# A decoder on one core: where the operands of the matrix products lie in SBUF, by pads between pools and wider rows

## The chip, the core and the metric

The kernel runs on one core of a Trainium2 chip. The metric is the time of one execution on the device in microseconds (us); of several executions the median is taken, and less is better. The core has five engines that the text names: TensorE (PE, with its weight loads as PEld), VectorE (DVE), ScalarE (ACT), GpSimd (POOL) and the DMA queue of SyncE (SP). SBUF is the on-chip memory of 128 partitions; a tile occupies the same byte addresses in each of its partitions, and "address" below means the byte address within a partition.

## The reference, cut to what matters

A sequence of 256 tokens of width 1024 goes through four decoder layers (differential attention, latent attention, dilated attention, differential attention, each followed by a gated feed-forward), a norm, and then two layers of a second kind, each a mix of pooling, convolution and sparse attention followed by a feed-forward with a short convolution. Nearly all of the arithmetic is products of activations with weight matrices in float32:

```
for i in range(DEPTH):
    h = rms_norm(x, attn_norm[i])
    mix = attention(h, ...)                       # one of three kinds
    x = x + mix
    x = x + swiglu(rms_norm(x, ffn_norm[i]), f_w_gu[i], f_w_out[i])
...
for l in range(DEPTH_2):
    mix = token_mix(h, ...)
    h = layer_norm(DEEPNORM_ALPHA * h + mix, ln1_g[l], ln1_b[l])
    ffn = conv_ffn(h, w_up[l], ffn_dw_w[l], ffn_dw_b[l], w_down[l])
    h = layer_norm(DEEPNORM_ALPHA * h + ffn, ln2_g[l], ln2_b[l])
```

The second kind's pooling divides windowed sums over 2, 4, 8 and 16 tokens by the number of tokens in the window, which is below the window's width only for the first 15 tokens.

## The kernel before

**Products.** Activations lie transposed, 128 channels by 256 tokens, in eight chunks. Each float32 operand is split into a high and a low part of the type float32r, and a product is three matmuls (`mm3`, L287): high by high, high weights by low activations, low weights by high activations. A matmul holds one operand of 128x128 in the array (the weights in the sense of the PE, loaded by an LDWEIGHTS of its own before each matmul) and streams the other, the moving operand, through it. In most products (`smode`, `smode2`) the model's weights are the held operand and 256 columns of activations move. In `mmode` it is the other way round: 128 tokens of activations are held, and 288 to 512 columns of weights move.

**Operands.** Weights come by `weights` (L295): a DMA of SP brings a piece of up to 128x1024 into `raw`, ACT rounds it into `whi`, DVE subtracts into `wlo` (L308); five buffers of `raw` and six each of `whi` and `wlo` of 4096 bytes rotate. The moving activations are of three kinds. The input of a layer's first products is split into `xh` and `xl` (L382 and L383), each a tile of eight rows of 258 columns, so that row k begins 1032*k bytes into the tile; 256 columns hold x, two more hold a gain and a bias for the early products of `normed` (258 columns wide). Results between products (attention outputs, the hidden rows of the feed-forwards) lie in slots of the pool `big` (tile `s4`, in the trace `s`), four rows of 256 columns each. The pooled and the convolved rows of `token_mix` (`pp` and `cc`, L1555 and L1637) lie in the pool `wk` under the tag `pl`, two rows of 256 columns in a tile.

**Where they lie.** The pools lie one behind the other in the order in which `Program.__init__` opens them (const, w, big, wk, and then the pools of some layers), the tiles of a pool one behind the other, each rounded up to 32 bytes. In the compiled program, taken modulo 512: `xh` begins at 160, so row k at 160+8k; `xl` at 224, so row k at 224+8k; all buffers of `raw`, `whi` and `wlo` at 192; all slots of `big` at 192; the pool `wk` at 192; its tag `pl` at 384. Slices of the weights are whole multiples of 512 bytes into their tile, but for the two weights 288 and 328 columns wide. The distance of a moving operand behind the held one is therefore -32+8k for `xh`, 32+8k for `xl`, 0 for the slots, and 192 for `pp` and `cc`.

**Order.** The instructions of the woven stretches (attention, token mixing) keep an order that a small planner in the program writes out with assumed durations (`US`, L29); addresses don't enter it. Feed-forwards and output projections run as they are written: PE through one block of weights after the other.

**Small things that the change touches.** `pk1` (L405) holds constants, among them `cnt` (2x256 columns), the reciprocal window counts that POOL multiplies in at L1532. `acc` (L1121) sums the moments of the norms, `ang` and `angn` (L1335 and L1338) are the rope's angles in the pool `wk`; the pool `mix` (`self.own`, L1326) is opened for the second kind of layers.

Of the kernel before, what the change touches and what calls it, by code (L numbers as in the profile page):

```python
# [10 lines left out]
F32 = mybir.dt.float32  # L11
R = mybir.dt.float32r
# [7 lines left out]
S = 256  # L20
# [8 lines left out]
US = {256: 0.12, 288: 0.132, 328: 0.155, 384: 0.175, 512: 0.235}  # L29
POOLED = (5, 7)  # L30
NH = 18
WARM = 10
NORM, POOL = (7, 8, 9), 8
FILL = -3.0e38
# [39 lines left out]
class Pack:  # L74
    def __init__(self):
        self.at, self.parts, self.n = {}, [], 0
# [25 lines left out]
def prepare(i):  # L102
    f = lambda a: np.asarray(a)
# [45 lines left out]
    p = Pack()  # L149
# [28 lines left out]
    nat = np.arange(S)  # L178
# [2 lines left out]
    p.add("ropeC", rope_tab(500000.0, 16, sigma()))  # L181
    inv = (10000.0 ** (-np.arange(32, dtype=np.float64) / 32)).astype(np.float32)
    p.add("inv", np.tile(inv[None], (128, 1)))
    cnt = np.zeros((128, 2, S), np.float32)
    for g, win_ in enumerate((2, 4, 8, 16)):
        cnt[(g % 2) * 64:(g % 2) * 64 + 64, g // 2] = np.float32(1) / np.minimum(nat + 1, win_).astype(np.float32)
    p.add("cnt", cnt.reshape(128, 2 * S))
    a["pack"] = np.concatenate(p.parts, axis=1)

    sg = sigma()  # L190
    q, k = sg[:, None], sg[None, :]
# [4 lines left out]
    for t in range(2):  # L196
        h = slice(t * 128, t * 128 + 128)
# [14 lines left out]
class Program:  # L212
    def __init__(self, tc, ins, out, at):
        self.tc, self.nc, self.ins, self.out, self.at = tc, tc.nc, ins, out, at
        self.ready = []
        self.woven, self.now, self.queue, self.inside, self.serial = False, 0.0, [], False, 0
        with ExitStack() as ctx:
            pool = lambda n, b, **k: ctx.enter_context(tc.tile_pool(name=n, bufs=b, **k))
            self.const = pool("const", 1)
            self.wp = pool("w", 3)  # L220
            self.big = pool("big", 12)
            self.wk = pool("wk", 2)
            self.ps = pool("ps", 2, space=bass.MemoryType.PSUM)
            self.pool = pool
            self.main()
# [140 lines left out]
    def setup(self):  # L366
        nc, c = self.nc, self.const
        i = self.ins
        self.x = []
        self.pk0 = c.tile([128, PK0], F32, name="pk0")  # L370
        nc.scalar.dma_start(self.pk0, i["pack"][:, :PK0])
        self.x4 = []
        for h in range(2):
            x = c.tile([128, 4, 256], F32, name=f"x{h}")
            nc.sync.dma_start(x, i["xT"][h])
            if h == 0:
                self.ready.append(self.weights(i["w_aqk"][0, 0, 0], 512))
            self.x4.append(x)
            self.x += [x[:, k, :] for k in range(4)]
            self.x2 = getattr(self, "x2", []) + [x[:, k:k + 2, :] for k in (0, 2)]  # L380
        self.ident = self.col("ident", 0, 128)
        self.xh = c.tile([128, 8, 258], R, name="xh")  # L382
        self.xl = c.tile([128, 8, 258], R, name="xl")  # L383
        self.identr = c.tile([128, 128], R, name="identr")
        nc.vector.tensor_copy(self.identr, self.ident)
        self.ones = c.tile([128, 1], F32, name="ones")
        nc.vector.memset(self.ones, 1.0)
        self.onesd = c.tile([128, 1], F32, name="onesd")
        nc.vector.memset(self.onesd, 1.0 / D)
        self.onesq = c.tile([128, 128], F32, name="onesq")  # L390
        nc.vector.memset(self.onesq, 1.0 / 512)

        self.woven = True
        ps = self.tp_bank()[:, :128]
        for _ in range(WARM):
            self.matmul(ps, self.onesq, self.onesq, start=True, stop=True)
        self.woven = False
        warm = c.tile([128, 1], F32, name="warm")
        self.act(warm, self.ones)
        self.nhalf = c.tile([128, 8], F32, name="nhalf")  # L400
        nc.vector.memset(self.nhalf, -0.5)
# [716 lines left out]
    def moments(self, k, chunk, accs, eng):  # L1118

        if k == 0:  # L1120
            accs.append(self.wk.tile([128, 256], F32, name="acc", tag="acc", bufs=3))  # L1121
            eng.tensor_copy(accs[0], chunk)
        elif k < 7:
            eng.tensor_add(accs[0], accs[0], chunk)  # L1124
        else:
            accs.append(chunk)
# [92 lines left out]
    def early(self, st):  # L1219

        h, l = self.xh, self.xl
        st["z"] = [(h[:, k, :], l[:, k, :]) for k in range(8)]
        for n, name in ((256, st["g"]), (257, st["b"])):
            v = self.col(name, 0, 8)
            self.act(h[:, :, n], v)
            self.nc.vector.tensor_sub(l[:, :, n], v, h[:, :, n].bitcast(F32))
# [95 lines left out]
    def angles(self):  # L1324
        nc = self.nc
        c = self.own = self.pool("mix", 1)  # L1326
        self.causal = c.tile([128, 384], F32, name="causal")
        nc.scalar.dma_start(self.causal, self.ins["causal"])
        pi = c.tile([128, 2], I32, name="posi")
        nc.scalar.dma_start(pi, self.ins["pos"])  # L1330
        pf = c.tile([128, 2], F32, name="posf")
        nc.vector.tensor_copy(pf, pi)
        inv = self.col("inv", 0, 32)
        wk = self.wk
        ang = wk.tile([128, 2, 32], F32, name="ang", bufs=1)  # L1335
        for t in range(2):
            nc.vector.tensor_scalar(ang[:, t, :], inv, pf[:, t:t + 1], None, op0=OP.mult)
        n = wk.tile([128, 2, 32], F32, name="angn", bufs=1)  # L1338
        magic = 12582912.0
        nc.vector.tensor_scalar(n, ang, float(1.0 / (2 * math.pi)), magic, op0=OP.mult, op1=OP.add)  # L1340
        nc.vector.tensor_scalar(n, n, -magic, None, op0=OP.add)
        c1 = 6.28125
        c2 = float(np.float32(2 * math.pi - c1)) 
        c2 = float(np.float32(np.frombuffer(np.uint32(np.frombuffer(np.float32(c2).tobytes(), np.uint32)[0] & 0xFFFFF000).tobytes(), np.float32)[0]))
        c3 = float(np.float32(2 * math.pi - c1 - c2))
        flat = lambda a: a.rearrange("p a b -> p (a b)")
        for cc in (c1, c2, c3):
            self.stt(flat(ang), flat(n), -cc, flat(ang), OP.mult, OP.add)
        lim = 3.1415925
        nc.vector.tensor_scalar(ang, ang, lim, -lim, op0=OP.min, op1=OP.max)  # L1350

        self.rt = c.tile([128, 2, 128], F32, name="rt")
        self.act(self.rt[:, :, 96:128], ang, AF.Sin)
        nc.vector.tensor_scalar(self.rt[:, :, 64:96], self.rt[:, :, 96:128], -1.0, None, op0=OP.mult)
        self.act(n, ang, AF.Abs)
        nc.vector.tensor_scalar(n, n, -1.0, float(math.pi / 2), op0=OP.mult, op1=OP.add)
        self.act(self.rt[:, :, 0:32], n, AF.Sin)
        nc.vector.tensor_copy(self.rt[:, :, 32:64], self.rt[:, :, 0:32])
        self.onesc = c.tile([128, 128], F32, name="onesc")
        nc.vector.memset(self.onesc, 1.0 / 256)  # L1360
        self.pw = c.tile([128, 2, 2, 64], F32, name="pw")
        nc.scalar.dma_start(self.pw, self.ins["pool_w"])
        self.bd = c.tile([128, 2, 128], F32, name="bd")
        nc.vector.memset(self.bd, 0.0)
        self.cvp = c.tile([128, 2, 286], F32, name="cvp")
        nc.vector.memset(self.cvp, 0.0)
        self.zk = [c.tile([128, 2, 256], F32, name=f"zk{n}") for n in range(2)]
        for t in self.zk:
            nc.gpsimd.memset(t, 0.0)
        self.hb = c.tile([128, 2, 26], F32, name="hb")  # L1370
        for l in range(2):
            nc.vector.tensor_scalar(self.hb[:, l, 0:2], self.col(f"bc{l}", 2, 2), 0.5, None, op0=OP.mult)
            nc.vector.tensor_scalar(self.hb[:, l, 2:26], self.col(f"bg{l}", 0, 24), 0.5, None, op0=OP.mult)

    def token_mix(self, l, st):
        nc, wk, i = self.nc, self.wk, self.ins
# [138 lines left out]
        s1 = wk.tile([128, 2, 256], F32, name="pl1", tag="pl", bufs=4)  # L1515
        gp = nc.gpsimd
# [11 lines left out]
        shifted(s0, s1, al, 1, 4)  # L1528
        gp.tensor_copy(s1[lo_, 1, :], s0[lo_, 1, :])
        shifted(s1, s0, hi_, 1, 8)  # L1530
        cnt = self.col("cnt", 0, 512).rearrange("p (f n) -> p f n", f=2)
        gp.tensor_mul(s1, s1, cnt)  # L1532
        gp.tensor_sub(s1, s1, u)
        cvp = self.cvp
        for f in range(2):
# [109 lines left out]
        for f in range(8):  # L1645
# [3 lines left out]
            for s in range(2):  # L1649
                g = gate(3 * f + s)  # L1650
# [3 lines left out]
        for hf in range(2):  # L1654
            w = self.weights(i["w_ato"][l, hf], 512)
            for ff in range(4):
                f = hf * 4 + ff
                ps = self.mm_bank()[:, :256]
                self.smode(ps, w, 0, 4, ff * 128, os_, True, True)
                g = gate(3 * f + 2)  # L1660
# [4 lines left out]
        chunk, st = self.deepnorm(f"ln1_g{l}", f"ln1_b{l}", True)  # L1665
# [3 lines left out]
    def conv_ffn(self, l, st, more):  # L1669
# [9 lines left out]
        for j in range(FC):  # L1679
# [15 lines left out]
            nc.vector.tensor_mul(h, s, u[:, 1, :])  # L1695
            self.split(hs[j][0], hs[j][1], h, 1.0, nc.gpsimd if j < NH else None)
        chunk, st = self.deepnorm(f"ln2_g{l}", f"ln2_b{l}", more)
# [34 lines left out]
```

## Time and profile before

| what | value |
|---|---|
| median of 3 runs | 2299.73 us (2299.43 to 2301.78) |
| profiled execution, its own time | 2302.48 us |
| its span in the trace | 2300.7 us |
| mean granted TensorE clock | 0.985 of 2.4 GHz |
| PE busy | 2226.4 us (97%) |
| DVE busy | 1625.7 us (71%) |
| ACT busy | 1325.1 us (58%) |
| POOL busy | 148.2 us (6%) |
| moved by DMA | 365.93 MB, mean 159 GB/s |

The end of a matmul in the trace is modelled and neighbours overlap, so neither a matmul's duration nor PE's busy share tells how fast the products follow each other. That is read from the starts: the time from the first start to the last, divided by the number of matmuls between, is called the pitch below.

### The profile page before, as it was taken

What the parts mean: (1) busy time and instruction counts of PE and PEld (TensorE: products, weight loads), DVE (VectorE), ACT (ScalarE), POOL (GpSimd) and SP (SyncE); (2) the same over time, 40 slices, a digit from 0 to 9 for tenths busy, and PEclk for the clock granted to TensorE, in tenths of its full rate; (3) what the DMA queues carried; (4) which work ended last, traced back from release to release, by engine and by line L of the source; (5) the groups of instructions that cost most, each with busy time, mean ns of one, the idle gap of its engine ahead of it and who ended that gap; (6) DMA issues with size and microseconds to landing.
All of it is one profiled execution on the core that took longest, in us unless ns stands there. A gap on an engine that the chain in (4) does not pass through costs nothing.

```text
span 2300.7 us, 42530 instructions
## 1 busy us (share of the span) xinstructions
PE 2226.4 (97%) x16676; PEld 2100.6 (91%) x16676; DVE 1625.7 (71%) x2940; ACT 1325.1 (58%) x2378; POOL 148.2 (6%) x167
## 2 busy tenths in 40 slices
PE   9999998999999999999999999989989998998998
PEld 7899997999977778999978999889989998998998
DVE  7776666766556656766677766796888689778875
ACT  7764457544556655644587545645566564656653
POOL 0000000100000000000000001010012011001211
PEclk9999999999999999999999999999999999998999
DMA  6345563355554343455633655534445544443643
GB/s 243 124 155 185 155 184 118 124 189 157 184 193 138 110 138 129 147 184 160 208 125 111 211 169 175 174 136 140 169 139 198 157 153 156 169 161 123 212 155 103
DMA packets 111801, 365.93 MB, mean 159 GB/s; under 512 B 12528, under 2 KB 14704, under 8 KB 111600
## 3 DMA queue, kind: packets, MB, share of 16 engines
q1 hardware_dynamic: 109728, 360.17, 47.6%
q10 hardware_dynamic: 1728, 2.78, 0.4%
q8 instruction: 131, 2.15, 0.4%
q14 instruction: 70, 0.57, 0.1%
q0 software_dynamic: 144, 0.26, 0.1%
HBM read 362.38 MB, written 1.05 MB: 158 GB/s over the span
## 4 chain that ended last, share of the span: by engine, by line
PE 72%; DVE 6%; ACT 4%; issue 1%; DMA 0%; POOL 0%; ACTq 0%; DVEq 0%; POOLq 0%
PE mm L265 62%; PE sc L265 6%; PE tp L319 2%; DVE wlo L308 1%; ACT whi L236 1%; PE tp L265 1%; ACT xh L236 1%; ACT s L236 1%; ACT x L236 1%; DVE score L1481 0%; PE tp L1135 0%; PE tp L728 0%; DVE mx L1480 0%; DVE gut L239 0%; DVE acc L1124 0%
## 5 line engine op out<-in xcount | busy, mean ns | idle before, releaser
L308 DVE TENSOR_TENSOR wlo<-raw,whi 128x1024 fp32r<-128x1024 f32 (+3 forms) x752 | 844.7, 1127 | 355.8 <-ACT whi L236 352.7
L236 ACT ACTIVATE whi<-raw 128x1024 fp32r<-128x1024 f32 (+3 forms) x752 | 731.8, 978 | 589.0 <-PE mm L265 368.5
L265 PE MATMUL mm<-xh,wlo 128*128 128x256 f32 x2496 | 706.5, 283 | 16.5 <-DVE wlo L308 16.5
L265 PE MATMUL mm<-xh,whi 128*128 128x256 f32 x2496 | 713.1, 286 | 0.3 <-ACT whi L236 0.3
L265 PE MATMUL mm<-xl,whi 128*128 128x256 f32 x2496 | 705.5, 283 | 0.4 <-DVE xl L1185 0.3
L265 PE MATMUL mm<-s,whi 128*128 128x256 f32 x2944 | 538.1, 284 | 0.0
L265 PEld LDWEIGHTS mm<-xh,wlo 128*128 128x128 f32 x2496 | 474.6, 190 | 17.4 <-DVE wlo L308 17.4
L265 PEld LDWEIGHTS mm<-xh,whi 128*128 128x128 f32 x2496 | 475.7, 191 | 2.8 <-issue 1.0
L265 PEld LDWEIGHTS mm<-xl,whi 128*128 128x128 f32 x2496 | 475.4, 191 | 1.5 <-DVE xl L1185 0.8
L265 PEld LDWEIGHTS mm<-s,whi 128*128 128x128 f32 x2944 | 460.3, 192 | 2.2 <-issue 1.1
L265 PE MATMUL mm<-s,wlo 128*128 128x256 f32 x1472 | 416.9, 283 | 0.0
L265 PEld LDWEIGHTS mm<-s,wlo 128*128 128x128 f32 x1472 | 282.3, 192 | 0.0
L265 PE MATMUL mm<-whi,xh 128*128 128x512 f32 (+2 forms) x592 | 238.4, 404 | 8.0 <-ACT whi L236 4.5
L265 PE MATMUL mm<-wlo,xh 128*128 128x512 f32 (+2 forms) x592 | 233.9, 395 | 3.5 <-DVE wlo L308 3.5
L265 PE MATMUL mm<-whi,xl 128*128 128x512 f32 (+2 forms) x592 | 232.6, 393 | 0.0
L265 PEld LDWEIGHTS mm<-whi,xh 128*128 128x128 f32 x592 | 113.3, 192 | 30.8 <-ACT whi L236 5.2
L265 PEld LDWEIGHTS mm<-wlo,xh 128*128 128x128 f32 x592 | 113.6, 192 | 24.0 <-DVE wlo L308 4.8
L265 PEld LDWEIGHTS mm<-whi,xl 128*128 128x128 f32 x592 | 113.2, 191 | 22.1
L236 ACT ACTIVATE s<-guh 128x256 fp32r<-128x256 f32 x132 | 54.8, 416 | 100.2 <-DVE guh L552 93.6
L504 POOL TENSOR_TENSOR rstd<-ms,nhalf 128x2 f32<-128x2 f32 x29 | 29.0, 1000 | 1070.0 <-DVE ms L502 1061.5
L548 DVE TENSOR_TENSOR gut<-mm,rbc 128x512 f32<-128x512 f32 x88 | 60.4, 691 | 40.9 <-PE mm L265 40.9
L239 DVE SCALAR_TENSOR_TENSOR gut<-mm,pk,gut 128x255 f32<-128x255 f32 (+1 forms) x160 | 76.1, 477 | 6.1 <-ACT gut L236 3.8
(326 smaller groups left out, 2502.1 us busy)
## 6 DMA issues: line engine op xcount, KB each, us to landing
raw<-w_gu SPq DMA_DIRECT2D x176, 512.0 KB, 3.8
raw<-w_up SPq DMA_DIRECT2D x88, 512.0 KB, 4.0
raw<-w_zs SPq DMA_DIRECT2D x60, 512.0 KB, 4.7
raw<-w_out SPq DMA_DIRECT2D x64, 384.0 KB, 3.2
raw<-w_cqk SPq DMA_DIRECT2D x48, 512.0 KB, 4.3
raw<-w_out SPq DMA_DIRECT2D x64, 320.0 KB, 2.8
raw<-w_aqk SPq DMA_DIRECT2D x32, 512.0 KB, 4.5
raw<-w_cv SPq DMA_DIRECT2D x24, 512.0 KB, 4.0
```

The costliest lines, as they stand in the source:

```text
L236: return self.nc.scalar.activation(out, in_, func, bias=bias, scale=scale, **kw)
L239: return self.nc.vector.scalar_tensor_tensor(out, a, s, b, op0=op0, op1=op1)
L265: i = self.nc.tensor.matmul(*a, **kw)
L308: e.tensor_sub(lo, raw, hi.bitcast(F32))
L319: i = self.nc.tensor.transpose(out, in_, self.ident if ident is None else ident)
L504: self.powered = [self.nc.gpsimd.tensor_tensor(r, ms, self.nhalf[:, :n], op=OP.pow).ins]
L548: nc.vector.tensor_mul(t, ps, rb[:, None, :].to_broadcast([128, 2, 256]))
```

## The change

A tile `padx` of 56 columns (224 bytes) in the pool const ahead of `xh`, and three pools of one unused tile each: 72 columns (288 bytes) ahead of the weights, 48 (192 bytes) ahead of the slots, 80 (320 bytes) ahead of `wk`. The rows of `xh` and `xl` become 384 columns (1536 bytes, three times 512) apart; 258 of them are used as before. `cnt` shrinks to 17 columns per half and POOL's multiplication is made in two parts (16 columns one by one, 240 by the last column broadcast); `acc` moves to the pool `mix`, `ang` and `angn` to the rotating tag `t1`. No product is added, left out or reordered in the program's text.

```diff
+PADS = (56, 72, 48, 80)
...
-    cnt = np.zeros((128, 2, S), np.float32)
+    cnt = np.zeros((128, 2, 17), np.float32)
...
             self.const = pool("const", 1)
+            pad = lambda n, cols: pool(n, 1).tile([128, cols], F32, name=n)
+            pad("padw", PADS[1])
             self.wp = pool("w", 3)
+            pad("padb", PADS[2])
             self.big = pool("big", 12)
+            pad("padk", PADS[3])
             self.wk = pool("wk", 2)
...
-        self.xh = c.tile([128, 8, 258], R, name="xh")
-        self.xl = c.tile([128, 8, 258], R, name="xl")
+        c.tile([128, PADS[0]], F32, name="padx")
+        self.xh = c.tile([128, 8, 384], R, name="xh")
+        self.xl = c.tile([128, 8, 384], R, name="xl")
...
-            accs.append(self.wk.tile([128, 256], F32, name="acc", tag="acc", bufs=3))
+            accs.append(self.own.tile([128, 256], F32, name="acc", tag="acc", bufs=3))
...
-        st["z"] = [(h[:, k, :], l[:, k, :]) for k in range(8)]
+        st["z"] = [(h[:, k, :258], l[:, k, :258]) for k in range(8)]
...
-        ang = wk.tile([128, 2, 32], F32, name="ang", bufs=1)
+        ang = self.t1("ang", (2, 32))
...
-        n = wk.tile([128, 2, 32], F32, name="angn", bufs=1)
+        n = self.t1("angn", (2, 32))
...
-        cnt = self.col("cnt", 0, 512).rearrange("p (f n) -> p f n", f=2)
-        gp.tensor_mul(s1, s1, cnt)
+        cnt = self.col("cnt", 0, 34).rearrange("p (f n) -> p f n", f=2)
+        gp.tensor_mul(s1[:, :, :16], s1[:, :, :16], cnt[:, :, :16])
+        gp.tensor_mul(s1[:, :, 16:], s1[:, :, 16:], cnt[:, :, 16:].to_broadcast([128, 2, 240]))
```

## Rows read from the trace of the kernel before

**Rows 1.** Page, part 1: busy time, share of the span, instructions.
```profile
span 2300.7 us, 42530 instructions
PE 2226.4 (97%) x16676; PEld 2100.6 (91%) x16676; DVE 1625.7 (71%) x2940; ACT 1325.1 (58%) x2378; POOL 148.2 (6%) x167
```

**Rows 2.** Page, part 4: the chain that ended last, by engine.
```profile
PE 72%; DVE 6%; ACT 4%; issue 1%; DMA 0%; POOL 0%; ACTq 0%; DVEq 0%; POOLq 0%
```

**Rows 3.** Pieces of that chain: start us, us, engine, tile, line, instructions.
```profile
437.72 8.94 PE mm L265 x75
...
451.32 169.82 PE mm L265 x1424
...
1271.89 144.74 PE mm L265 x1215
...
2257.04 30.60 PE mm L265 x255
```

**Rows 4.** Stretches: us, engines' busy time (instructions), clock, DMA share, GB/s.
```profile
150.00:300.00 150.00, 150.00 (x1261) 150.00 (x1261) 97.77 (x132) 72.83 (x108) 0.00 (x0) 1.00 0.56 177
1702.00:1840.00 138.00, 137.94 (x1142) 137.79 (x1143) 107.75 (x168) 82.14 (x135) 21.47 (x17) 0.99 0.57 186
```

**Rows 5.** Page, part 5, groups of products: busy us, mean ns, idle before.
```profile
L265 PE MATMUL mm<-xh,wlo 128*128 128x256 f32 x2496 | 706.5, 283 | 16.5 <-DVE wlo L308 16.5
...
L265 PE MATMUL mm<-s,whi 128*128 128x256 f32 x2944 | 538.1, 284 | 0.0
...
L265 PE MATMUL mm<-s,wlo 128*128 128x256 f32 x1472 | 416.9, 283 | 0.0
```

**Rows 6.** Groups by shape, PE, smaller products: busy us, mean ns, idle before.
```profile
L265 PE MATMUL sc<-s,whi 128*128 128x256 f32 x220 | 43.1, 294 | 2.6 <-ACT s L236 1.7 <-DVE s L239 0.5 <-ACT blat L236 0.4
...
L265 PE MATMUL sc<-s,wlo 128*128 128x256 f32 x110 | 31.3, 284 | 0.0
L265 PE MATMUL sc<-xl,whi 128*128 128x258 f32 x96 | 29.9, 311 | 0.0
...
L265 PE MATMUL mm<-pp,whi 128*128 128x256 f32 x64 | 11.7, 276 | 0.0
...
L265 PE MATMUL mm<-pp,wlo 128*128 128x256 f32 x32 | 8.8, 276 | 0.0
```

**Rows 7.** Timeline of PE, second kind's first output stage: `pp` and `cc`.
```profile
1627.84 0.39 PE L265 MATMUL mm<-cc,whi 128*128 128x256 f32 x2
...
1630.10 0.28 PE L265 MATMUL mm<-pp,wlo 128*128 128x256 f32 x1
```

**Rows 8.** Timeline of PE, same stage, some 6 us on: slots.
```profile
1634.10 0.40 PE L265 MATMUL mm<-s,whi 128*128 128x256 f32 x2
...
1636.50 0.28 PE L265 MATMUL mm<-s,wlo 128*128 128x256 f32 x1
```

**Rows 9.** Timeline of PEld in the stretch of rows 7: weight loads.
```profile
1628.07 0.30 PEld L265 LDWEIGHTS mm<-cc,whi 128*128 128x128 f32 x2
1628.29 0.19 PEld L265 LDWEIGHTS mm<-cc,wlo 128*128 128x128 f32 x1
```

**Rows 10.** Groups by shape, PE: products with 512 moving columns of weights.
```profile
L265 PE MATMUL mm<-whi,xh 128*128 128x512 f32 x544 | 222.8, 411 | 8.0 <-ACT whi L236 4.5 <-ACT s L236 2.3 <-ACT qtok L236 1.1
```

**Rows 11.** Waits of PE: for whom, us in total, times, longest.
```profile
PE mm L265 <- DVE wlo L308: 20.0, 6, 6.3
PE tp L1135 <- DVE acc L1124: 5.4, 2, 2.7
```

**Rows 12.** POOL's count multiplication (L1532): duration min/median/max, starts.
```profile
L1532 POOL TENSOR_TENSOR pl<-pl,pk x2: 1214/1215/1216, 1516.7 to 1934.4; 128x512 f32<-128x512 f32 x2
```

**Rows 13.** The tile `angn` on DVE and ACT: first and last use.
```profile
L1340 DVE TENSOR_SCALAR angn<-ang x1: 179/179/179, 1254.1 to 1254.1; 128x64 f32<-128x64 f32 x1
...
L236 ACT ACTIVATE rt<-angn x1: 242/242/242, 1260.9 to 1260.9; 128x64 f32<-128x64 f32 x1
```

More of the change, by code (lines that the diff above doesn't have):

```diff
@@ L183, in prepare @@
     p.add("inv", np.tile(inv[None], (128, 1)))
-    cnt = np.zeros((128, 2, S), np.float32)
+    cnt = np.zeros((128, 2, 17), np.float32)
     for g, win_ in enumerate((2, 4, 8, 16)):
-        cnt[(g % 2) * 64:(g % 2) * 64 + 64, g // 2] = np.float32(1) / np.minimum(nat + 1, win_).astype(np.float32)
-    p.add("cnt", cnt.reshape(128, 2 * S))
+        cnt[(g % 2) * 64:(g % 2) * 64 + 64, g // 2] = np.float32(1) / np.minimum(nat[:17] + 1, win_).astype(np.float32)
+    p.add("cnt", cnt.reshape(128, 34))
     a["pack"] = np.concatenate(p.parts, axis=1)
```

## The prediction

> **What bounds the kernel now.** I read the page's busy times first: PE stands at 97%, DVE at 71%, ACT at 58%, POOL at 6% [rows 1]. Matmul ends are modelled, so 97% alone proves little; the chain of waits settles it: 72% of the span is PE's, 6% DVE's, 4% ACT's [rows 2]. The chain taken in order of time shows where: it runs through PE alone in long pieces, the longest 169.82 us with 1424 matmuls [rows 3]. I counted the pieces of 8.9 us or longer whose matmuls follow each other in under 123 ns: there are 13, with 8299 matmuls, the first and the last in [rows 3]; the chain as shown begins only at 376 us, so the first layer's feed-forward comes from the stretches, 1261 matmuls in 150 us with PE busy throughout and DVE busy 97.77 of 150 us [rows 4]. In these 9560 matmuls nothing but PE's own pace sets the time. What a matmul costs there is the pitch: 144.74 us / 1215 = 119.1 ns where mostly `xh` and `xl` move, 30.60 us / 255 = 120.0 ns where only slots move [rows 3].
>
> **The row that matters.** One stage of the kernel before has both addresses of the change side by side. In the output stage of the first token mixing, `pp` and `cc` lie 192 bytes behind the weights: the starts run from 1627.84 to 1630.10 us, which is 20 matmuls in 2.26 us, 113.0 ns [rows 7]. Six us later slots move at a distance of 0, with the same shape, the same line, the same kind of weight tile: 1634.10 to 1636.50 us, 20 matmuls in 2.40 us, 120.0 ns [rows 8]. Weight loads go on beside the stream in either case (one begins every 0.11 us) [rows 9], so a held operand is read while a moving one is, and the distance between their addresses can matter. I take 113.3 ns for the distance 192 (the printed starts are rounded to 10 ns; the whole run of rows 7 repeats every 0.34 us per three matmuls).
>
> **The change part by part.** First, where things end up. `padx` puts `xh` from 160 to 160+224 = 384 (modulo 512), and with rows of 1536 bytes all eight rows, and those of `xl`, stand at 384. The pool const grows by 224 + 2*4032 bytes and loses 1920 of `cnt`, 6368 in all; with the pad of 288 the weights move by 6656 = 13*512 and stay at 192. The pad of 192 puts the slots at 384, the pad of 320 leaves `wk` at 192 (7168 = 14*512 in all) and `pl` at 384. So every product with 256 moving columns of activations gets the distance 192 that `pp` and `cc` have now; the scores and transposes keep theirs, but for some short ones.
>
> Gain at most. `xh` and `xl` move in 3 * (2496 + 96) = 7776 matmuls [rows 5, 6], at 119.1 - 113.3 = 5.8 ns each: 45.1 us. Slots move in 2944 + 1472 + 220 + 110 = 4746 [rows 5, 6], at 120.0 - 113.3 = 6.7 ns: 31.8 us. Together 76.9 us over 12,522 matmuls.
>
> What of it reaches the end. Of the 9560 matmuls of the stretches in which PE alone sets the time, some 260 are `pp` and `cc` (192 in all, as both have the counts of [rows 6]) and wide ones, so 9300 of 12,522, 74%, give their gain in full: 56.9 us. The other 26% (20.0 us) lie in woven attention and token mixing, where PE waits now and then for DVE and ACT; with PE's 72% of the whole chain I take half, 10.0 us. Does the feed keep up at the new pace? The tightest long stretch is the second kind's feed-forward, with DVE busy 107.75 of 138 us [rows 4]; if PE needs 5.3% less time there, DVE is busy 107.75 of some 131 us, 82%, and the DMA's 186 GB/s become 196 at a share of 0.60 in place of 0.57; I count no loss but keep it as a rival. PE's waits for `wlo` are 20.0 us in six places [rows 11], at the starts of stages; they neither grow nor shrink.
>
> The products of `mmode` change too, and no row shows their new distance: weights at 192 move and activations at 384 are held, which is 512 - 192 = 320. There are 544 with `whi` and `xh`, three times as many in all, 1632 [rows 10]. Nearest are the gains of the narrow products, so I bound each by 6.7 ns either way: 10.9 us, half of it on the path, -5.5 to +5.5 us. I take 0, because nothing in the trace says on which side 320 lies.
>
> The rest is small. POOL's multiplication of 1.215 us [rows 12] becomes two of together the same columns; bounds from nothing to another 1.2 us per layer, on an engine that is idle 94% of the time, and the rows are wanted by PE only with a step queued 34 us later. If that cover were gone, it would be 2.4 us. `acc` keeps its three buffers; PE waits 5.4 us for it in two places [rows 11] and that stays. `ang` and `angn` take two of the six `t1` buffers from 1254 to 1261 us [rows 13]; a later user could wait for them at most those 7 us and has four other buffers first: 0. The smaller `pk1` takes a quarter megabyte off a DMA at the start: 0. No wait is added to any queue.
>
> Sum: 56.9 + 10.0 = 66.9 us, from a profiled span of 2300.7 us to 2233.8 (2235.6 us by that execution's own time of 2302.5). The median of the runs before is 2.8 us under the profiled execution's time, so against the median: 2299.7 - 66.9 = 2232.8, which I give as **2233 us**.
>
> **The rivals.** *No effect.* The pace of `pp` and `cc` comes from something else in their stage, and distance does nothing. For it: they are only 192 products, in two places. Against it: [rows 7, 8] are 6 us apart, on the same engines' work. It gives 2300 us; chance 0.08. The Trainium skill speaks for this rival: "SBUF — State Buffer", section "Who interferes with whom", gives PE two independent read ports, one for the moving operand and one for LDWEIGHTS, and says that PE never waits on anyone. By that rule both pitches would be equal and the sum would be 0; the trace has 113.0 against 120.0 ns [rows 7, 8] and does not agree.
>
> *Slower.* The same premise, and in addition the present drift of 8 bytes from row to row is what makes `xh` (119.1 ns) faster than the slots (120.0 ns) [rows 3]. With all rows at one distance `xh` and `xl` would then go at the slots' pace: 7776 * 0.9 ns = 7.0 us more, 2307 us. It decides from the point at which the distance 192 brings less than 0.9 ns. The chance is 0.06.
>
> *Feed-bound.* DVE's splitting of the weights becomes the bound in the second kind's layers, where it is busiest [rows 4]. Then some 3400 of the 9300 free-running matmuls gain nothing, 20.8 us, and the woven stages' 10.0 us fall away as well: 36.1 us are left, 2264 us. For it stands DVE's 78% in that stretch; against it, that PE doesn't wait for `wlo` inside it [rows 11]. The chance is 0.10.
>
> *More.* All of the 76.9 us arrive, and the wide products gain 5.5 us: 2217 us, chance 0.06.
>
> **How the numbers follow.** The forecast of 2233 us has 0.70, with a range of its own from 2222 to 2247 (woven part all or none, wide products at either bound). The range of 8 in 10 takes in "more" and "feed-bound" and leaves out the 0.14 of no effect and slower, with a little of each tail: 2217 to 2265 us. A measurement of this kernel tells about 0.2% (4.6 us) from no change. Faster: 0.70 + 0.10 + 0.06 = 0.86; within 0.2%: 0.08; slower: 0.06.
>
> **What would show it.** Right: in the timeline after, starts of three `mm` products of `s` lie 0.34 us apart and not 0.36; those of `xh` and `xl` the same; a piece of the chain such as that of 1215 matmuls takes some 138 us; DVE's busy time is unchanged, its share higher; `pp` and `cc` are as before. Wrong: slots still at 120 ns (no effect); PE waiting for `wlo` in the middle of feed-forwards (feed-bound); pieces of twelve 512-column products that leave the present pace by more than 0.08 us. If only slots or only `xh` gain, one of the two address sums above is wrong.

## The result and the profile after

The changed kernel takes 2274.01 us in the median of 4 executions (2267.26 to 2279.07), beside 2299.73 before: a ratio of 0.988 with an interval of 0.986 to 0.991. A later series of the same program gives 2271.9 (2266.07 to 2272.88) beside 2298.64, 0.987 (0.985 to 0.989). It is faster by some 26 us, or a little over 1%, where 67 were forecast. Its executions spread over 12 us in the first series and 7 in the second, those of the kernel before over 2.4 us in the first and over 6 and 9 in later ones (2297.13 to 2303.46 and 2297.05 to 2305.66).

The page of the profiled execution (its own time 2279.07 us) shows the same balance as [rows 1, 2]:

```profile
span 2277.3 us, 42526 instructions
PE 2200.4 (97%) x16676; PEld 2077.3 (91%) x16676; DVE 1624.8 (71%) x2940; ACT 1325.4 (58%) x2378; POOL 147.4 (6%) x169
...
PE 72%; DVE 7%; ACT 4%; issue 1%; POOL 0%; ACTq 0%; DVEq 0%; POOLq 0%
```

The pieces of the chain answer to [rows 3] (start us, us, engine, tile, line, instructions; the program's line 265 is now 270):

```profile
448.40 167.73 PE mm L270 x1424
...
743.40 2.77 PE mm L270 x12
...
1262.01 143.12 PE mm L270 x1215
...
1690.40 130.54 PE mm L270 x1135
1821.59 30.04 PE mm L270 x255
...
2099.39 135.47 PE mm L270 x1135
2235.48 28.93 PE mm L270 x255
```

The last four lines are two pairs of stages with the same code and the same addresses. The first pair runs at 130.54 / 1135 = 115.0 and 30.04 / 255 = 117.8 ns per matmul, the second at 119.4 and 113.5. Cut to their inside, from 1700 to 1800 and from 2110 to 2210 us, the first and the third are

```profile
1699.90 100.19 PE mm L270 x884
...
2109.90 100.11 PE mm L270 x850
```

or 113.3 and 117.8 ns. Products at a distance of 192 bytes thus have two paces, and either one lasts through a whole stage. In the long stretches of `xh`, `xl` and the slots (240 matmuls or more without a pause) 1390 of 8693 matmuls ran at 113.3 ns, all others at 117.8. The two paces differ in the weight loads (PEld, busy us, mean ns; the first fence is the fast stretch 1700 to 1800 us, the second the slow one 460 to 560 us):

```profile
L270 PEld LDWEIGHTS mm<-xh,wlo 128*128 128x128 f32 x265 | 49.7, 188 | 0.0
L270 PEld LDWEIGHTS mm<-xl,whi 128*128 128x128 f32 x264 | 49.5, 188 | 0.0
L270 PEld LDWEIGHTS mm<-xh,whi 128*128 128x128 f32 x264 | 49.5, 188 | 0.0
```

```profile
L270 PEld LDWEIGHTS mm<-xh,wlo 128*128 128x128 f32 x283 | 54.3, 192 | 0.0
L270 PEld LDWEIGHTS mm<-xl,whi 128*128 128x128 f32 x284 | 53.3, 188 | 0.0
L270 PEld LDWEIGHTS mm<-xh,whi 128*128 128x128 f32 x283 | 53.1, 188 | 0.0
```

At 113.3 ns no load takes 192 ns; at 117.8 every third does; in the kernel before, where slots at 0 run at 120.0, all do:

```profile
L265 PEld LDWEIGHTS mm<-s,whi 128*128 128x128 f32 x279 | 43.6, 192 | 0.0
L265 PEld LDWEIGHTS mm<-s,wlo 128*128 128x128 f32 x139 | 26.7, 192 | 0.0
```

### The profile page after: what moved, and what is told of

The parts are those of the page before. It is cut to its first block, busy times and chain, and to the rows that moved or that the text cites. A ratio compares the mean times of both kernels' runs of the same rounds, so it can differ in the third digit from the quotient of the medians.

```text
span 2277.3 us, 42526 instructions
## 1 busy us (share of the span) xinstructions
PE 2200.4 (97%) x16676; PEld 2077.3 (91%) x16676; DVE 1624.8 (71%) x2940; ACT 1325.4 (58%) x2378; POOL 147.4 (6%) x169
## 4 chain that ended last, share of the span: by engine, by line
PE 72%; DVE 7%; ACT 4%; issue 1%; POOL 0%; ACTq 0%; DVEq 0%; POOLq 0%
PE mm L270 62%; PE sc L270 6%; PE tp L324 3%; DVE wlo L313 1%; ACT whi L241 1%; PE tp L270 1%; ACT xh L241 1%; ACT s L241 1%; ACT x L241 1%; PE tp L1141 0%; DVE score L1487 0%; DVE mx L1486 0%; PE tp L734 0%; DVE gut L244 0%; DVE acc L1130 0%
## 5 line engine op out<-in xcount | busy, mean ns | idle before, releaser
L270 PE MATMUL mm<-s,whi 128*128 128x256 f32 x2944 | 524.4, 281 | 0.2 <-DVE s L244 0.2
L270 PEld LDWEIGHTS mm<-s,whi 128*128 128x128 f32 x2944 | 450.7, 188 | 2.6 <-issue 1.1
L270 PE MATMUL mm<-s,wlo 128*128 128x256 f32 x1472 | 412.3, 280 | 0.0
L270 PEld LDWEIGHTS mm<-whi,xh 128*128 128x128 f32 x592 | 113.4, 192 | 29.9 <-ACT whi L241 5.0
L270 PEld LDWEIGHTS mm<-whi,xl 128*128 128x128 f32 x592 | 113.5, 192 | 22.0
```

Source lines behind the costliest of these rows:

```text
L270: i = self.nc.tensor.matmul(*a, **kw)
```

## The experiments

Theory: the distance decides which paces are possible, and what PE did just before decides which of them a stretch falls into. Rivals: the gain comes from the even rows of `xh` and `xl`; the pace of a stage is set by what DVE, ACT and the DMAs do in it; the choice is chance alone; the pace goes by the address of the moving operand alone, as the weights begin at 192 in every run. All distances are modulo 512; each kernel keeps the other edits of the change unless its diff says more. Single executions are named as such.

**All distances 0** (`d0_0`).

```diff
-PADS = (56, 72, 48, 80)
+PADS = (8, 120, 0, 0)
```

> All of the change but the distances: xh, xl and the slots 0 bytes behind the weights (rows of 384 columns, acc, ang, cnt as changed). Theory 'rhythm' (the distance decides which rhythms of 113.3 and 120.0 ns per product are possible, and at 0 only the slow one is): all 256-column products at 120.0 ns, so xh and xl lose 1.1 ns each against 118.9 before, 7776 x 1.1 = 8.6 us, 2308 us. Theory 'rows' (the gain of the changed kernel comes from the even rows of xh and xl, not from a distance): xh and xl at 117.8 ns as in the changed kernel, slots at 120.0, 2291 us.

Measured: 2302.74 us beside 2295.57 (one execution of each). Stretches of `xh` and `xl`, then of slots:

```profile
959.93 100.08 PE mm L270 x834
...
1074.89 50.16 PE mm L270 x418
```

Both are 120.0 ns. The time alone would not tell, as single executions of the kernel before lie between 2295.57 and 2305.66 us; the chain does, with its longest piece at 170.88 us, against 169.82 before [rows 3] and 167.73 with the change:

```profile
450.47 170.88 PE mm L270 x1424
```

So even rows at distance 0 make `xh` and `xl` slower than before, by about what the forecast's slower rival said; "rows" falls, and the other edits cost nothing that can be seen.

**Other distances**, `xh` and `xl` first, then the slots (`d64_128`, `d320_256`, `d448_384`, and then `d96_32` and `d160_224`).

```diff
-PADS = (56, 72, 48, 80)
+PADS = (24, 104, 32, 96)
...
+PADS = (88, 40, 64, 64)
...
+PADS = (120, 8, 96, 32)
...
+PADS = (32, 96, 8, 120)
...
+PADS = (48, 80, 56, 72)
```

> xh and xl 64 bytes behind the weights, slots 128 bytes. Theory 'rhythm': each long stretch runs at 113.3, 117.8 or 120.0 ns and at nothing between; at 64 and 128 bytes nothing is known, a single rhythm per distance if it leaves no choice. Theory 'load' (113.3 or 117.8 ns in the changed kernel is set by what DVE, ACT and the DMAs do in the stage): pitches between those steps, and in the same stages the same order (feed-forward of the first kind slow, stages at 1690 to 1820 us and 2235 to 2265 us fast). Time between 2233 us (all 113.3) and 2308 us (all 120.0).

> xh and xl 320 bytes behind the weights, slots 256 bytes; the wide products' weights are then 192 behind the held activations. 'Rhythm': each long stretch at 113.3, 117.8 or 120.0 ns, other distances than 192 may leave one rhythm alone; 'load': the stages keep the pitches of the changed kernel in order. If the sign of the distance doesn't matter, 320 (= -192) gives xh and xl a mix of 113.3 and 117.8 as 192 does. Time between 2233 and 2308 us.

> xh and xl 448 bytes behind the weights, slots 384 bytes. 'Rhythm': stretches at 113.3, 117.8 or 120.0 ns only; if the conflict is one of nearness in the ring of 512 bytes, 448 (64 before the weights) is the slowest, near 120.0, and 384 like 128. 'Load': the stages keep the pitches of the changed kernel in order. Time between 2233 and 2308 us.

> xh and xl 96 bytes behind the weights, slots 32 bytes. Of the earlier distances the odd multiples of 64 (64, 192, 320, 448) gave 113.3 or 117.8 ns, the even ones 118.7 or 120.0 (0 and 256 only 120.0). Theory 'halves of 128 bytes' (conflict when both operands are in the same half of 128 bytes as they stream): 96 lies on the side of 64 and 128 alike and gives a rhythm between, 32 one at or near 120.0. Theory 'steps of 64' (only whole steps of 64 bytes count, rounded down): 96 like 64 (113.3 or 117.8), 32 like 0 (120.0).

> xh and xl 160 bytes behind the weights, slots 224 bytes. 'Steps of 64, rounded down': 160 like 128 (118.7 or 120.0), 224 like 192 (113.3 or 117.8). 'Halves of 128': both between, the same for both sides of 192. If one of them runs at 113.3 ns in every stretch, it is the distance to take.

Measured, one execution each: 2278.69, 2295.08 and 2269.87 us beside 2295.57; 2296.08 and 2289.98 beside 2298.64. Paces of long stretches, from the pieces of the chain between the same bounds:

| distance | what moved | us / matmuls | ns | also seen in long stretches |
|---|---|---|---|---|
| 0 | `xh`, `xl` | 100.08 / 834 | 120.0 | nothing else |
| 32 | slots | 53.20 / 456 | 116.7 | 117.8 (22.14 / 188) |
| 64 | `xh`, `xl` | 95.20 / 840 | 113.3 | 117.8 (100.11 / 850) |
| 96 | `xh`, `xl` | 100.08 / 834 | 120.0 | nothing else |
| 128 | slots | 50.08 / 422 | 118.7 | 120.0 |
| 160 | `xh`, `xl` | 90.11 / 768 | 117.3 | 118.7 |
| 224 | slots | 50.17 / 424 | 118.3 | between 118 and 119 |
| 256 | slots | 50.04 / 417 | 120.0 | nothing else |
| 320 | `xh`, `xl` | 100.23 / 851 | 117.8 | 113.3, in two short stretches |
| 384 | slots | 45.12 / 376 | 120.0 | 118.7 (45.09 / 380) |
| 448 | `xh`, `xl` | 90.10 / 795 | 113.3 | 117.8 (95.05 / 807) |

Two of these rows in the trace, `d64_128` in two feed-forwards:

```profile
949.89 95.20 PE mm L270 x840
...
1259.98 100.11 PE mm L270 x850
```

Distance does matter, and more finely than by steps of 64: odd multiples of 64 can run at 113.3 ns, even ones never did, 96 is as slow as 0. But no distance tried holds 113.3 by itself; each one with that pace also has 117.8. The readings of the distance put on record fail: 116.7, 117.3, 118.3 and 118.7 ns are none of the three paces of "rhythm"; by "steps of 64" 96 would go like 64 and 32 like 0; by "halves of 128" 32 would be near 120.0; by nearness in the ring 448 would be slowest. "Load" isn't borne out here: `d64_128` has the feed-forward at 950 us fast and the one at 1260 us slow, with the same code, and the changed kernel had both slow.

The address of the moving operand alone does not set the pace either. In the attention's scores both operands lie in slots, so they stand at distance 0 wherever the slots lie. Twelve of them with the first of the products behind them, in the changed kernel (slots at 384) and in the one before (slots at 192):

```profile
111.66 1.60 PE L270 MATMUL sc<-s,s 128*128 128x256 f32 x12
113.10 0.28 PE L270 MATMUL mm<-s,wlo 128*128 128x256 f32 x1
```

```profile
112.38 1.60 PE L265 MATMUL sc<-s,s 128*128 128x256 f32 x12
113.82 0.28 PE L265 MATMUL mm<-s,wlo 128*128 128x256 f32 x1
```

Either way it is 1.44 us for twelve, 120.0 ns, while products of the same slots at 384 with weights at 192 run at 117.8 or 113.3. These are short pieces, so this is a strong sign and not more.

**The changed kernel again** (`after_again`, no edit).

> The changed kernel once more, unchanged. Theory 'restart' (at 192 bytes two rhythms are possible, 113.3 and 117.8 ns, and each restart of PE after a pause falls into one of them by small differences in time): the long stretches that ran fast (1695 to 1820 us, 2236 to 2262 us) and slow (152 to 322, 450 to 620, 950 to 1121, 1263 to 1435 us) are dealt anew, and single times lie between 2233 us (all fast) and 2283 us (all 117.8). Theory 'load' (what the other engines and the DMAs do in a stage sets its rhythm): the same stretches are fast and slow as in the first profile, and single times agree within 0.2%.

Measured: 2271.9 us, 0.987. The four stages at the end once more:

```profile
446.04 167.73 PE mm L270 x1424
...
1255.58 143.12 PE mm L270 x1215
...
1678.96 131.66 PE mm L270 x1135
1811.28 28.92 PE mm L270 x255
2090.13 130.54 PE mm L270 x1135
2221.32 30.03 PE mm L270 x255
```

The third stage ran 135.47 us in the first profile and 130.54 here, the second 30.04 and 28.92, the fourth 28.93 and 30.03. One program, one set of addresses, another deal: "load" falls, as far as it means a fixed pace per stage. The dealing isn't even, though: the long feed-forwards of the first kind of layer were slow in both. In all, 2767 of the 8693 matmuls of long stretches ran fast here.

The two profiled executions are 13.0 us apart, and not all of that is the dealing. The piece of 1215 matmuls begins 6.4 us earlier here, though every long stretch ahead of it ran at 117.8 ns in both. A part of the difference goes with the granted clock, as from 615 to 660 us: 0.92 in the first profile, 1.00 here.

```profile
615.00:660.00 45.00, 42.47 (x210) 35.83 (x209) 24.06 (x30) 27.78 (x38) 1.53 (x1) 0.92 0.55 184
```

```profile
615.00:660.00 45.00, 42.47 (x212) 35.64 (x211) 24.67 (x29) 28.76 (x40) 1.53 (x1) 1.00 0.60 191
```

**Only the slots at 192** (`s_only`).

```diff
-PADS = (56, 72, 48, 80)
+PADS = (0, 96, 48, 80)
...
-        c.tile([128, PADS[0]], F32, name="padx")
-        self.xh = c.tile([128, 8, 384], R, name="xh")
-        self.xl = c.tile([128, 8, 384], R, name="xl")
+        self.xh = c.tile([128, 8, 258], R, name="xh")
+        self.xl = c.tile([128, 8, 258], R, name="xl")
```

> Only the slots are moved to 192 bytes behind the weights; xh and xl keep rows of 258 columns at 160 and 224 (distances -32+8k and 32+8k). xh and xl at 118.9 ns as before. Theory 'restart, entered from drifting rows': pp and cc ran at 113.4 ns in both places of the kernel before, where they follow xh and xl without a pause, so the slots, which follow them in every feed-forward, fall into the fast rhythm too: 4746 x 6.6 = 31 us less, 2269 us. Theory 'restart, dealt by chance': a mix of 113.3 and 117.8 ns, 4746 x 2.2 to 6.6, 10 to 31 us less, 2269 to 2290 us.

Measured: 2277.06 us beside 2298.64, 0.989 (0.987 to 0.992). Three pieces: `xh` and `xl`; slots that follow them without a pause; slots that follow a pause of PE (the norm's estimate after the third output chunk, L1148):

```profile
959.98 90.12 PE mm L270 x758
...
1057.98 54.06 PE mm L270 x477
...
1405.93 20.14 PE mm L270 x171
```

They run at 118.9, 113.3 and 117.8 ns. So it was in all six feed-forwards: slots behind drifting rows (rows 8 bytes further on, one after the other) at 113.3, and all three stretches behind that pause at 117.8. "Entered from drifting rows" held behind rows and not behind a pause, and its 2269 us was 8 too low. This is the entry that `pp` and `cc` had in the kernel before. It also shows what `xh` and `xl` at 192 take away: in the changed kernel the slots follow rows at 192, and keep the slow pace of these.

**A break in every block** (`kick_24_88`): row 7 of `xh` and `xl` back at its old distances, 24 and 88. The lines left out write the row where it is now read; DVE and ACT have some more and shorter instructions for it.

```diff
+        self.oh = [86 if k in (7,) else 0 for k in range(8)]
+        self.ol = [102 if k in (7,) else 0 for k in range(8)]
...
-        return [(self.xh[:, k, :256], self.xl[:, k, :256]) for k in range(8)]
+        return [(self.xh[:, k, self.oh[k]:self.oh[k] + 256], self.xl[:, k, self.ol[k]:self.ol[k] + 256]) for k in range(8)]
```

> The changed kernel, but for row 7 of xh and xl, which begins 86 and 102 columns on, so that it stands 24 and 88 bytes behind the weights, as it does in the kernel before; rows 0 to 6 and the slots stay at 192. Theory 'entry' (which of the two rhythms a stretch at 192 runs in depends on what came right before: after a pause mostly 117.8, after rows at other distances 113.3): six of every 48 matmuls of the feed-forwards' first half are such a row, so rows 0 to 6 and the slots that follow run at 113.3 ns, only slots after a pause at 117.8; 7776 matmuls at some 114.3 and 4746 at some 113.9, against 117.1 and 117.0: 22 + 15 us less than the changed kernel, some 2237 us. Theory 'chance': mixes of 113.3 and 117.8 as in the changed kernel, 2266 to 2285 us.

Measured: 2249.43 us (2245.9 to 2255.46) beside 2302.69, a ratio of 0.978 (0.976 to 0.981), the fastest of all and ahead of both kernels. In the profile (2245.9 us) the pieces, with those of a single feed-forward's first half and of its slots behind them:

```profile
441.26 162.56 PE mm L270 x1424
...
1794.85 28.92 PE mm L270 x255
...
2201.80 30.03 PE mm L270 x255
```

```profile
934.97 100.13 PE mm L270 x875
...
1045.97 52.13 PE mm L270 x460
```

114.4 ns in the first half with the breaks in it, 113.3 in the slots behind it, and so in all six feed-forwards; slots behind a pause are still dealt (28.92 and 30.03). That is what "entry" expected; its 2237 us was 12 too low: it took the breaks at 1.0 ns a matmul, close to the 1.1 measured, but counted every gain in full, where 87% was the prediction's own share, and the rest is not accounted for.

**A small break** (`kick_200`), **two odd steps in turn** (`xl64`), **448 ahead of 192** (`d448_192`).

```diff
+        self.oh = [2 if k in (7,) else 0 for k in range(8)]
+        self.ol = [2 if k in (7,) else 0 for k in range(8)]
...
-        return [(self.xh[:, k, :256], self.xl[:, k, :256]) for k in range(8)]
+        return [(self.xh[:, k, :256], self.xl[:, k, 96:352]) for k in range(8)]
...
+PADS = (120, 8, 48, 80)
```

> As the one before, but row 7 of xh and xl stands 200 bytes behind the weights, 8 more than the other rows. 'Entry': if any break of the even distance does it, rows 0 to 6 and the slots after them run at 113.3 ns, some 2237 us; if it takes a break to another step of 64 bytes, nothing changes, 2266 to 2285 us as the changed kernel.

> xh at 192, xl at 64 bytes behind the weights (xl begins 96 columns into its rows), slots at 192. Both are distances that gave 113.3 or 117.8 ns. 'Entry': the alternation is a break within each three matmuls and the stretches run at 113.3 ns, 2240 us; if an alternation between two odd steps of 64 changes nothing, a mix of 113.3 and 117.8, 2266 to 2285 us.

> xh and xl at 448 bytes behind the weights, slots at 192. xh and xl ran at 113.3 ns in four of six long stretches at 448, and in one or two of six at 192. 'Entry': slots follow xh and xl without a pause and take on their rhythm: 113.3 where these ran at 113.3; some 2255 us with four of six. 'Chance': slots independent of what xh and xl did just before.

Measured, one execution each beside 2302.69: 2259.2, 2281.2 and 2261.26 us. The first two kernels' feed-forward at 960 to 1110 us (first the break of 8 bytes, then the alternation), and for `d448_192` a slow and a fast one:

```profile
959.93 150.16 PE mm L270 x1273
```

```profile
959.99 150.05 PE mm L270 x1274
```

```profile
959.94 150.17 PE mm L270 x1275
...
1269.89 120.13 PE mm L270 x1060
```

A break of 8 bytes does not always work: 118.0 ns here, with all its breaks, though slots in four of the six feed-forwards came out at 113.3. This kernel has the same additional instructions of DVE and ACT as `kick_24_88`, so these are not what brings the fast pace. The alternation of 192 and 64 does not work at all, 117.8 in nearly all stretches. In `d448_192` the pieces run over from `xh` and `xl` into the slots, 117.8 in the one and 113.3 in the other: here the pace passes from one distance to another where there is no pause. It does not always do so. In `d64_128` rows at 64 ran at 113.3 ns and `pp` and `cc` at 192, right behind them, at 117.8, although both distances allow both paces:

```profile
1589.91 8.16 PE mm L270 x72
...
1598.99 10.13 PE mm L270 x86
```

So it was in both token mixings there, and in both of `d320_256`; behind rows at 0 or 96, which ran at 120.0, `pp` and `cc` ran at 113.3 every time. What comes before thus matters in either direction, but does not settle the pace alone: in `xl64`, behind rows at 117.8, `pp` and `cc` ran at 117.8 in one token mixing and at 113.3 in the other. Which entries lead to the fast pace, and what decides it behind a pause, stays open: of the twelve stretches of slots behind the pause in the feed-forwards of `after`, `after_again`, `s_only` and `kick_24_88`, five ran at 113.3 and seven at 117.8.

## Why the prediction was wrong

**The step that failed** is "I take 113.3 ns for the distance 192". The rows were right and the reading of them was not: [rows 7] show one of two paces, and all 192 products of `pp` and `cc` entered it in the same way, straight from rows at other distances. The changed kernel shows it on the row itself: `pp` and `cc` were not moved, and in the first token mixing, behind slow rows at 192, they ran at 117.8 ns (10.13 us / 86), in the second, behind fast ones, at 113.4 (10.09 us / 89):

```profile
1607.89 10.13 PE mm L270 x86
...
2016.98 10.09 PE mm L270 x89
```

The prediction's sign "`pp` and `cc` are as before" did not come. The moved operands entered from a pause, or from one another, and mostly came out at 117.8. The two gains of the sum were 5.8 and 6.7 ns; at the slow pace they are 119.1 - 117.8 = 1.3 and 120.0 - 117.8 = 2.2 ns. All slow, the sum would have been 7776 x 1.3 + 4746 x 2.2 = 20.5 us, of which the forecast's own share of 87% reaches the end: 17.9 us, 2282 us. All fast it was 2233. (Two small slips of the working change nothing here. The piece of 119.1 ns holds some 260 products of slots, and drifting `xh` and `xl` alone run at 118.9, as in `s_only`: 1.6 us less in the sum. The forecast's own range, with both its terms at their bounds, is 2217 to 2248 and not 2222 to 2247.) Every execution lies between, 2266.07 to 2279.07, and the medians at about a fifth of the way. The counts of fast matmuls agree, as an estimate: 16% in the first profile and 32% in the second make 2277 and 2269 us from the profiled 2302.48, and these executions took 2279.07 and 2266.07.

**What held.** The bound: PE alone in the long stretches. Matmul by matmul the pieces of [rows 3] became shorter (169.82 to 167.73 us, 144.74 to 143.12). The share of 87% isn't contradicted: with it the counts come to within about 3 us of both profiles. The addresses: the paces of `d0_0`, `s_only` and the others changed where their sums put the operands. The feed: in the fast stretch from 1695 to 1818 us PE is busy throughout with DVE at 100.09 of 123 us, 81%, against the 82% worked out, so "feed-bound" did not come:

```profile
1695.00:1818.00 123.00, 123.00 (x1088) 123.00 (x1087) 100.09 (x155) 77.07 (x126) 17.95 (x16) 1.00 0.60 195
```

PE's waits for `wlo` are 20.1 us in six places, for `acc` 5.4 in two, as in [rows 11]:

```profile
PE mm L270 <- DVE wlo L313: 20.1, 6, 6.3
PE tp L1141 <- DVE acc L1130: 5.4, 2, 2.7
```

The wide products went from 231.7 to 230.8 ns (2.78 and 2.77 us for twelve), within the bounds and near the 0 taken. POOL's multiplication, 1.215 us in [rows 12], became 286 + 1114 ns, on an engine that nobody waits for there.

**The rivals.** "No effect" was refuted where it mattered most: with all distances at 0 the same kernel runs `xh`, `xl` and the slots at 120.0 ns throughout, and with the change at 113.3 and 117.8. By the page of the Trainium skill "SBUF — State Buffer", section "Who interferes with whom", PE's two read ports are independent and PE never waits on anyone, so this would not be. The traces don't agree: they show 113.3, 117.8 and 120.0 ns for the same work, and the granted clock was 1.00 in the fast stretch from 1695 to 1818 us and in the slow one from 450 to 570 us alike. "Slower" named about the right price for even rows (`d0_0`), behind a premise that did not hold. None of the rivals foresaw a distance with two paces; the forecast's list lacked "the row shows one of several states".

## What to carry to other kernels

A pace read in one place is the pace of that place and of its entry: before it is multiplied by thousands of instructions, look for the same configuration entered in another way, and where there is only one entry, let the range reach down to the case in which only some of them get it. Pieces of the chain with equal counts in every kernel make a table from which such states are read at a glance. And a change can take away what it does not touch: even rows at the good distance cost the slots the fast pace that drifting rows give them for nothing in `s_only`.

## What the runs showed of the hardware

In a dense stream of 256-column products with a weight load each, the pace takes few values, 113.3, 117.8, 118.7 and 120.0 ns at multiples of 64 bytes, and holds one for hundreds of matmuls until a pause or an operand elsewhere. At 113.3, 117.8 and 120.0 it goes with the weight loads: none, every third or all of them take 192 ns instead of 188. The distance in bytes between the moving and the held operand limits the choice (0, 96 and 256: 120.0 alone). Rows at 24 and 88 bytes right before the slots led these into the fast pace in six of six feed-forwards, in `s_only` and in `kick_24_88` alike; a pause led to the slow one in three cases of three in `s_only`, in one of three in `kick_24_88`, in seven of twelve with both executions of the changed kernel. That it is reads of the two operands that collide was argued, not shown: the runs show the dependence on the distance, no collision itself.
